# A hybrid RWKV/pooling layer on one core: block reads in four parts, one corner transposition, weights asked for seven tiles ahead

## The chip, the cores and the metric

The kernel runs on one core of one Trainium2 chip. The metric is the device time of one execution in microseconds; the median over runs is what is compared. Names used below: PE is TensorE (PEld its weight load), DVE is VectorE, ACT is ScalarE, POOL is GpSimd, SP is the sync engine, whose queue (SPq) issues nearly all transfers here; ACTq issues a few.

## The reference

One layer (DEPTH = 1) over 512 positions of width 2048, in float32:

```python
h = rms_norm(x, norm_g);  z = h @ w_in                  # 2048 -> 3200 + 1024 + 1024 + 1024 columns
zs = zs + (token_shift(zs) - zs) * mu                    # r, k, v, two low-rank inputs
decay = exp(-exp(-softplus(-(w0 + tanh(wd) @ w_up)) - 0.5));  a = sigmoid(a0 + ad @ a_up)
S_t = S_{t-1} (diag(w_t) - kk_t^T (a_t*kk_t)) + v_t^T k_t;  y_t = S_t r_t     # 16 heads x 64, 512 steps
y_rwkv = (head_group_norm(y) + bonus) * silu(g_rwkv)
y_pool = (trailing means over 2/4/8/16 - u) @ w_pool * pool_scale * silu(g_pool)
x = x + concat(y_rwkv, y_pool) @ w_out
x = x + sigmoid(x @ w_pg + b_pg) * (p @ w_ple)
out = rms_norm(x, final_g)
```

## The kernel before, in words

**Products.** Each large float32 product is made of three reduced-precision ones: `wsplit` reads a weight tile into `raw` (SP), ACT casts it to `whi` (line 132), DVE subtracts to get `wlo` (line 133), and PE multiplies `whi` by the high and the low part of the activations and `wlo` by the high part. The pools of `raw`, `whi` and `wlo` have four buffers each. One tile of `w_in` holds 4 x 128 rows by 128 columns and feeds 12 products of 512 columns.

**Weights' order.** `plan` lists all tiles in the order of use. `chunk(nm, c)` hands out one; each time it also calls `wsplit` for the two that follow it in `plan`. A scheduler in the compiler then sets the order on each engine: among what is ready it takes what the program wrote down first, except where `high_priority` lifts an instruction. PE keeps the program's order. `tc.issue_after(ins)` adds an order, without a wait, between `ins` and what the block puts on `ins`'s own engine.

**Stages.** First the norm and the transposition of x (to about 27 us). Then the middle stage (27 to 690 us): eight passes `j`, two heads each. In a pass, `recur(j)` walks eight chunks of 64 positions: the product `py` (state against queries), the sum `zs` on DVE, the product `pu`, copies `uv` on ACT, the product `ps`, the new state `sbd` on DVE. Between these links `pump` fills PE with the projections of the next passes and with the pool units (`zk`, `zr`, `zv`, `zg`, `zb`). Then the two projections with `w_out` and `w_pg` (690 to 1067 us) and the last norm.

**The block inverse.** While `recur(j)` runs, pass j+1 is prepared. After chunk 0, `scores(j + 1)` makes masked score blocks `mt`, writes the 32 x 32 diagonal blocks to DRAM (`nd`, four writes), and reads them back so that each of four groups of 32 partitions holds all of them: two tiles `n32`, rows 0 to 15 and rows 16 to 31 of the blocks, each with one read whose source is broadcast over four (line 682). Behind these on SP come the low-rank weights (`load_ab`), four reads of `bg` (128 KB each) and four of `vg` (64 KB each). `invert(j + 1)` solves the blocks in 31 short steps on DVE (`tm` line 709, `xw` line 713), two after each link from the second link of chunk 2 on; its first 16 steps need the first tile `n32` only. At its end it writes `xd` and reads it back into the corners of `x1` (four reads of 32 partitions, line 724).

**The corner.** `gather(j + 1)` turns the left half of `x1` in blocks of 32 x 32 on DVE, in two instructions of 32 partitions each (`y1`, line 777), and PE multiplies by the result (`pq`, 32 x 32 products). `turn_key` (chunk 7) needs `bg`, the transposition of `uv` in `gather` needs `vg`.

```python
        yt = [nc.vector.transpose(y1[pb:pb + 32], x1[pb:pb + 32, :, 0:32]) for pb in (0, 64)]
        ...
        units(lambda u, par, pb: mm(ps3[pb + 32:pb + 64, u, :],
                                                  mt[pb:pb + 32, par, u, 1 - par, 32:64],
                                                  y1[pb:pb + 32, u, :], start=True, stop=True,
```

Of the kernel before, what the change touches and what calls it, by code (L numbers as in the profile page):

```python
# [9 lines left out]
F32 = mybir.dt.float32  # L10
# [5 lines left out]
P = 128  # L16
# [8 lines left out]
NCH = T // C  # L25
# [9 lines left out]
def trunk_kernel(ctx: ExitStack, tc: tile.TileContext, x, p, norm_g, w_in, mu, w0, w_up, a0, a_up,  # L35
                 k_k, k_a, r_k, ln_w, ln_b, w_pool, pool_scale, w_out, w_ple, w_pg, b_pg, final_g, out):
    nc = tc.nc
    PSUM = bass.MemoryType.PSUM
    x, p, w_in, w_out, w_ple, w_pg = x[0], p[0, 0], w_in[0], w_out[0], w_ple[0], w_pg[0]
    out = out[0]  # L40
# [85 lines left out]

    def wsplit(src, kt, n, nm):
        raw = wp.tile([P, kt, n], F32, name=f"raw_{nm}", tag="raw")
        made = [nc.sync.dma_start(out=raw, in_=src)]
        hi = wp.tile([P, kt, n], F32R, name=f"whi_{nm}", tag="whi")  # L130
        lo = wp.tile([P, kt, n], F32R, name=f"wlo_{nm}", tag="wlo")
        made.append(nc.scalar.copy(hi, raw))  # L132
        made.append(nc.vector.tensor_tensor(lo, raw, hi.bitcast(F32), ALU.subtract))  # L133
        wmade[:] = made
        return hi, lo

    wmade = []

    def split(hi, lo, src):
        c_ = nc.scalar.copy(hi, src)  # L140
# [18 lines left out]
    def mm(*a, **k):  # L159
        i = nc.tensor.matmul(*a, **k)  # L160
        return tc.keep_in_program_order(i) if pin[0] else i
# [11 lines left out]
    plan, ready = [], {}  # L173
# [2 lines left out]
        for c in range(KT // CK):  # L176
            plan.append((nm, c, w_in[c * CK * P:(c + 1) * CK * P, c0:c0 + P].rearrange("(k p) n -> p k n", p=P), CK, P))

    def chunk(nm, c, ahead=2):
        while (nm, c) not in ready or ahead > 0:  # L180
            if (nm, c) in ready:
                ahead -= 1
            if not plan:
                break
            n_, c_, src, kt, w_ = plan.pop(0)
            if (n_, c_) not in ready:
                ready[n_, c_] = wsplit(src, kt, w_, f"{n_}_{c_}")
        return ready.pop((nm, c))

    yd = dram.tile([KT, P, T], F32, name="yd", bufs=1)  # L190
# [5 lines left out]
    n_ = 0  # L196
# [13 lines left out]
    for kind, nm, j in jobs:  # L210
# [7 lines left out]
        else:  # L218
            g, i = j // 4, j % 2
# [79 lines left out]
    for d in range(KT):  # L299
        xt_half(0, d)  # L300
        if d in WPOS:
            c = len(wl_)
# [18 lines left out]
    for g, win in enumerate(WINDOWS):  # L321
        t_ = cst.tile([P, win], F32, name=f"rc{g}")
# [21 lines left out]
    rw = s2a.enter_context(tc.tile_pool(name="rw", bufs=1))  # L344
# [6 lines left out]
    def load_ab(j):  # L351
        jc = slice(j * P, (j + 1) * P)
        w2 = []
        for nm, src in (("u", w_up), ("a", a_up)):
            raw = rw.tile([P, P], F32, name=f"{nm}r{j}", tag=f"l{nm}r")
            for h in range(2):
                nc.sync.dma_start(out=raw[64 * h:64 * h + 64, :], in_=src[0, :, jc])
            w2.append((raw, rw.tile([P, P], F32R, name=f"{nm}s{j}", tag=f"l{nm}s")))
        wab[j] = w2
# [24 lines left out]
    for nm, rows in (("u", slice(0, 64)), ("a", slice(64, 128))):  # L384
# [3 lines left out]
        t_ = rw.tile([P, T], F32R, name=f"{nm}hh")  # L388
# [10 lines left out]
    def zcols(ps, nm):  # L399
        for c in range(KT // CK):  # L400
            wh, wl = chunk(nm, c)
            for k in range(CK):
                kk = c * CK + k
                mm3(ps, wh[:, k, :], wl[:, k, :], hhi[:, kk, :], hlo[:, kk, :], kk == 0, kk == KT - 1)
                place[0] = 3 * (kk + 1)
                yield 3
# [107 lines left out]
                assert (nm, j) in zt  # L514
        return zt[nm, j]

    pws, kks, nrs, vgs, read, late = {}, {}, {}, {}, [], [None]

    H1, H2, H3, H4, H5, HE = 6, 12, 20, 8, 13, 40

# [34 lines left out]
    st_ = {}  # L555
# [3 lines left out]
    def prepare_key(j):  # L559
        k_ = need("k", j)  # L560
        kk = rw.tile([P, T], F32, name=f"kk{j}", tag="kk")
        nc.scalar.activation(kk, k_, AF.Square, scale=pc("k_k", j))
        kqh = rw.tile([P, T], F32R, name=f"kqh{j}", tag="t", bufs=4)
        kql = rw.tile([P, T], F32R, name=f"kql{j}", tag="t", bufs=4)
        split(kqh, kql, kk)
        kks[j] = (kk, kqh, kql)
# [25 lines left out]
    def scale_key(j):  # L592
        k_, kk = need("k", j), kks[j][0]
        if j < 2:
            nc.vector.reciprocal(kk, kk)
        nc.vector.scalar_tensor_tensor(kk, k_, pc("k_k", j), kk, ALU.mult, ALU.mult)
        kks[j] = kk
# [48 lines left out]
    def scores(j):  # L646
        ar, bk, v_ = (st_[j][n_] for n_ in ("ar", "bk", "v_"))
        kph, kpl = st_[j].pop("kp")

        mt = rw.tile([P, 2, 8, 2, C], F32, name=f"mt{j}", tag="mt", bufs=2)  # L650
        pm = [[psM.tile([P, T], F32, name=f"pm{j}_{par}0", tag="m"),
               psY.tile([P, T], F32, name=f"pm{j}_{par}1", tag="y")] for par in range(2)]
        for par in range(2):
            for q in range(4):
                for h in range(2):
                    rows = slice(64 * h, 64 * h + 64)
                    mm(pm[par][h][:, q * P:(q + 1) * P], bk[rows, q, 2 * par:2 * par + 2, :],
                       ar[rows, q, 2 * par:2 * par + 2, :], start=True, stop=True)
        for par in range(2):
            for h in range(2):  # L660
                nc.vector.tensor_tensor(mt[:, par, h::2, :, :],
                                        pm[par][h].rearrange("p (u a t) -> p u a t", u=4, a=2),
                                        msk[:, par:par + 2, :].unsqueeze(1).to_broadcast([P, 4, 2, C]), ALU.mult)


        ps = psM.tile([P, T], F32, name=f"pbo{j}", tag="m")
        mm(ps, blk, kph, start=True, stop=False)
        mm(ps, blk, kpl, start=False, stop=True)
        bv = rw.tile([P, T], F32, name=f"bv{j}", tag="bv", bufs=2)
        nc.vector.tensor_tensor(bv, ps, v_, ALU.mult)  # L670

        nd = dram.tile([2, 2, 8, 32, 32], F32, name=f"nd{j}", tag="nd")
        for par in range(2):
            pb = 64 * (1 - par)
            for b in range(2):
                rows = slice(pb + 32 * b, pb + 32 * b + 32)
                nc.sync.dma_start(out=nd[par, b].rearrange("u r c -> r u c"),
                                  in_=mt[rows, par, :, 1 - par, 32 * b:32 * b + 32])
        nb = []
        for i in range(2):  # L680
            t_ = rw.tile([P, 16, 32], F32, name=f"n32{j}_{i}", tag=("kk", "kp")[i])
            n_ = nc.sync.dma_start(out=t_, in_=nd[:, :, :, 16 * i:16 * i + 16, :].rearrange(
                "a b u r c -> (a b u) r c").unsqueeze(0).to_broadcast([4, 32, 16, 32]))
            nb.append(t_)
        if j + 1 < NJ:
            with tc.issue_after(n_.ins):
                load_ab(j + 1)
        bg = rw.tile([P, NCH, 4, 32], F32, name=f"bg{j}", tag="bk")
        with tc.issue_after(n_.ins):
            for q in range(4):  # L690
                nc.sync.dma_start(out=bg[32 * q:32 * q + 32],
                                  in_=st_[j]["bkd"].rearrange("(b k) (c q i) -> q k c b i", b=4, q=4, i=32)[q])
        if j:
            vg, vd = vgs[j]
            with tc.issue_after(n_.ins):
                for q in range(4):
                    nc.sync.dma_start(out=vg[32 * q:32 * q + 32],
                                      in_=vd.rearrange("(b k) (c q i) -> q k c b i", b=4, q=4, i=32)[q])
        st_[j].update(mt=mt, nb=nb, bv=bv, bg=bg)


# [28 lines left out]
    def gather(j):  # L730
# [8 lines left out]
        if j:  # L739
            vg, _ = vgs.pop(j)  # L740
# [26 lines left out]
        x1 = d["x1"]  # L767
# [6 lines left out]
        y1 = rw.tile([P, 8, 32], F32, name=f"y1{j}", tag="tm")  # L774

        with tc.issue_after(late[0].ins):
            yt = [nc.vector.transpose(y1[pb:pb + 32], x1[pb:pb + 32, :, 0:32]) for pb in (0, 64)]
        with tc.issue_after(yt[0].ins), tc.issue_after(yt[1].ins):
            if normed:
                normed.pop()()  # L780
            if j + 1 < NJ:
                scale_key(j + 1)
# [29 lines left out]
    def recur(j, work, between):  # L812
        d = st_.pop(j)
        pw, ar, mt, bv, uv, mv, x1 = (d[n_] for n_ in ("pw", "ar", "mt", "bv", "uv", "mv", "x1"))
# [5 lines left out]
        def step():  # L820
            hop[0] += 1
            if hop[0] > HS:
                with tc.issue_after(lead[0].ins):
                    for _ in range(HN + (hop[0] == HE1)):
                        next(work, None)
# [4 lines left out]
        for ch in range(NCH):  # L830
            par, q = ch % 2, ch // 2
            pb = 64 * (1 - par)
# [49 lines left out]
            if ch == NCH - 1:  # L882
                for c0 in range(0, NCH, 4):
                    py = pys[c0 // 4]
                    for qq in range(2):
                        for h in range(2):
                            for pr in range(2):
                                c_ = c0 + 2 * qq + pr
# [5 lines left out]
                    for pr in range(2):  # L894
                        yr = slice(64 * pr, 64 * pr + 64)
                        nc.scalar.copy(ysb[yr, c0 // 2:c0 // 2 + 2, :], py4[yr, pr::2, :])
            step()
            if j + 2 < NJ and ch == 4:
                prepare_key(j + 2)
            if ch == 0:  # L900
# [59 lines left out]
    prepare(0)  # L960
    pump(H3)
    scores(0)
    pump(H2)
    for _ in invert(0):
        pass
    pump(HT)
    gather(0)
    for j in range(NJ):
        def between():
# [5 lines left out]
        if j + 1 == NJ:  # L975
            pn.append(rw.tile([P, 2, T // 32, 32], F32, name="pn", tag="ar", bufs=2))
            for q in range(4):
                for c in range(2):
                    nc.sync.dma_start(out=pn[0][32 * q:32 * q + 32, c],
                                      in_=p[:, c * P + 32 * q:c * P + 32 * q + 32].rearrange("(b k) i -> k b i", k=32))  # L980
# [93 lines left out]
    for ec in range(D // EC):  # L1074
# [3 lines left out]
        for tt in range(NT):  # L1078
            rows = slice(tt * P, (tt + 1) * P)
            t_ = pp.tile([P, EC], F32, name=f"x2_{ec}_{tt}", tag=("u", "sw")[tt // 2])  # L1080
# [3 lines left out]
                                in_=t_.rearrange("p (c e) -> p c e", e=P))  # L1084
# [204 lines left out]
```

## Time and profile before

| what | value |
|---|---|
| median of 3 runs | 1072.54 us (1072.24 to 1074.22) |
| the profiled execution's own time | 1077.76 us |
| its span, first to last instruction | 1076.0 us |
| PE busy | 1047.7 us (97%) |
| DVE busy | 711.7 us (66%) |
| ACT busy | 435.0 us (40%) |
| mean granted TensorE clock | 0.997 |

The profile is one execution. A row of the timeline gives the start, the duration, the engine, the line and operation, what is written and read (without buffer numbers), how many alike were merged, and in brackets the idle time of the engine just before it and what ended that. A row of the waits gives the engine and line that waited, for whom, the total, the number of times and the longest. A row of the windows gives a stretch, the busy time of each engine in it with its instructions, the granted clock, the share of the 16 DMA engines that was busy, and GB/s.

### The profile page before, as it was taken

The page shows a single profiled execution, that of the slowest core. Times are in us where ns is not written, and L with a number is a line of the kernel's source. Part 1 is how long each engine was busy: PE and PEld are TensorE (multiplying, and loading weights), DVE is VectorE, ACT ScalarE, POOL GpSimd, SP SyncE. Part 2 cuts the span into 40 slices and gives each one's busy share as a digit, 9 for nine tenths or more (in the row PEclk, how much of TensorE's full clock was granted, in tenths as well). Part 3 has the DMA queues.
Part 4 walks back from the last instruction along what each step waited for, and adds up shares of the span by engine and source line. Part 5 has one row for each costly group of instructions (what it writes and reads, how often), then busy time and mean ns, then how long its engine had stood idle before and what let it go on. Part 6 is the DMA issues. An engine that isn't in the chain of part 4 may idle for free.

```text
span 1076.0 us, 17131 instructions
## 1 busy us (share of the span) xinstructions
PE 1047.7 (97%) x5912; PEld 864.6 (80%) x5912; DVE 711.7 (66%) x1879; ACT 435.0 (40%) x893; POOL 72.6 (7%) x180
## 2 busy tenths in 40 slices
PE   5999999999999999999999999999999999999996
PEld 4888878888877887888888788888888888888885
DVE  6676968878688689687786977464353344435356
ACT  7633424434334345253443344544232232324337
POOL 2100011010110110101101201000000000000000
PEclk9999999999999999999999999999999999999998
DMA  7434453453443544534544453775747659454534
GB/s 237 110 115 101 135 132 95 130 139 99 143 116 100 160 105 128 128 95 133 132 118 133 112 130 108 225 259 163 183 152 190 163 145 272 129 177 159 173 98 157
DMA packets 272733, 155.41 MB, mean 144 GB/s; under 512 B 114449, under 2 KB 235386, under 8 KB 272646
## 3 DMA queue, kind: packets, MB, share of 16 engines
q1 hardware_dynamic: 244630, 125.74, 42.2%
q10 hardware_dynamic: 28016, 28.58, 8.8%
q8 instruction: 46, 0.75, 0.3%
q14 instruction: 41, 0.34, 0.1%
HBM read 128.79 MB, written 24.95 MB: 143 GB/s over the span
## 4 chain that ended last, share of the span: by engine, by line
PE 81%; DVE 9%; DMA 5%; ACT 2%; issue 2%; SPq 1%; ACTq 0%; DVEq 0%
PE acc_o L160 16%; PE acc_g L160 16%; PE zb L160 10%; PE zv L160 7%; PE zr L160 7%; PE zg L160 6%; PE zk L160 6%; PE py L160 2%; PE pple L160 2%; DMA n<-nd 1%; PE pu L160 1%; PE pm L160 1%; DMA x<-xd 1%; PE pp L160 1%; PE ps L160 1%
## 5 line engine op out<-in xcount | busy, mean ns | idle before, releaser
L133 DVE TENSOR_TENSOR wlo_g<-raw_g,whi_g 128x512 fp32r<-128x512 f32 x84 | 57.1, 687 | 76.0 <-ACT whi_g L132 73.8
L160 PE MATMUL zb<-hhi,whi_b 128*128 128x512 f32 x256 | 105.5, 412 | 0.0
L160 PE MATMUL zb<-hhi,wlo_b 128*128 128x512 f32 x256 | 100.4, 392 | 0.0
L160 PE MATMUL zb<-hlo,whi_b 128*128 128x512 f32 x256 | 99.8, 390 | 0.0
L160 PE MATMUL acc_o<-wlo_o,yhi 128*128 128x512 f32 x256 | 99.6, 389 | 0.0
L160 PE MATMUL acc_o<-whi_o,ylo 128*128 128x512 f32 x256 | 99.6, 389 | 0.0
L133 DVE TENSOR_TENSOR wlo_o<-raw_o,whi_o 128x512 fp32r<-128x512 f32 x64 | 43.9, 690 | 81.0 <-ACT whi_o L132 72.8
L160 PE MATMUL acc_o<-whi_o,yhi 128*128 128x512 f32 x256 | 94.7, 389 | 0.0
L132 ACT CAST whi_g<-raw_g 128x512 fp32r<-128x512 f32 x84 | 51.9, 620 | 103.0 <-PE acc_g L160 57.4
L160 PE MATMUL acc_g<-whi_g,x2hi 128*128 128x512 f32 x208 | 81.1, 390 | 0.0
L160 PE MATMUL acc_g<-wlo_g,x2hi 128*128 128x512 f32 x208 | 81.0, 389 | 0.0
L160 PE MATMUL acc_g<-whi_g,x2lo 128*128 128x512 f32 x208 | 80.7, 390 | 0.0
L881 POOL TENSOR_SCALAR s0p<-sbd,pw 64x64 f32<-64x64 f32 x96 | 56.4, 587 | 336.6 <-DVE sbd L874 245.1
L132 ACT CAST whi_o<-raw_o 128x512 fp32r<-128x512 f32 x64 | 39.5, 621 | 96.1 <-PE acc_o L160 55.0
L132 ACT CAST whi_b<-raw_b 128x512 fp32r<-128x512 f32 x64 | 39.6, 620 | 75.9 <-PE zb L160 22.4
L713 DVE TENSOR_TENSOR xw<-xw,tm 128x60 f32<-128x60 f32 (+24 forms) x248 | 52.2, 210 | 7.1
L160 PEld LDWEIGHTS zb<-hhi,wlo_b 128*128 128x128 f32 x256 | 48.0, 188 | 10.8
L160 PEld LDWEIGHTS acc_o<-whi_o,ylo 128*128 128x128 f32 x256 | 48.1, 188 | 10.1
L160 PEld LDWEIGHTS acc_o<-whi_o,yhi 128*128 128x128 f32 x256 | 48.0, 188 | 10.0
L160 PEld LDWEIGHTS acc_o<-wlo_o,yhi 128*128 128x128 f32 x256 | 48.0, 188 | 9.9
L133 DVE TENSOR_TENSOR wlo_b<-raw_b,whi_b 128x512 fp32r<-128x512 f32 x64 | 43.7, 684 | 17.8 <-ACT whi_b L132 17.2
L160 PEld LDWEIGHTS zb<-hhi,whi_b 128*128 128x128 f32 x256 | 48.2, 188 | 8.6
(289 smaller groups left out, 2502.2 us busy)
## 6 DMA issues: line engine op xcount, KB each, us to landing
raw_b<-in_w_in_dram SPq DMA_DIRECT2D x64, 256.0 KB
raw_o<-in_w_out_dram SPq DMA_DIRECT2D x64, 256.0 KB
raw_g<-in_w_pg_dram SPq DMA_DIRECT2D x64, 256.0 KB
raw_k<-in_w_in_dram SPq DMA_DIRECT2D x32, 256.0 KB
raw_r<-in_w_in_dram SPq DMA_DIRECT2D x32, 256.0 KB
raw_v<-in_w_in_dram SPq DMA_DIRECT2D x32, 256.0 KB
raw_g<-in_w_in_dram SPq DMA_DIRECT2D x32, 256.0 KB
bkd<-bk SPq DMA_DIRECT2D x8, 512.0 KB
```

The costliest lines, as they stand in the source:

```text
L132: made.append(nc.scalar.copy(hi, raw))
L133: made.append(nc.vector.tensor_tensor(lo, raw, hi.bitcast(F32), ALU.subtract))
L160: i = nc.tensor.matmul(*a, **k)
L713: nc.vector.tensor_tensor(xw[:, 0:n_, s + 1:32], xw[:, 0:n_, s + 1:32], tm[:, 0:n_, 0:w_], ALU.add)
L881: nc.gpsimd.tensor_scalar(s0p[hc, :], nxt[hc, hc], pcn[hc], None, ALU.mult)
```

## The change

Four edits. (1) The read of each tile `n32` becomes four reads, one for each group of 32 partitions; only the first tile is read at once. (2) The second tile, `load_ab`, and the reads of `bg` and `vg` in pairs become portions: from pass 1 on, one is issued at the end of each chunk (chunks 1 to 6), all behind the first tile's last read on SP; in pass 0 they follow it directly. (3) `chunk` keeps the tile asked for and six more behind it in `ready`, so weights are written down seven tiles ahead in place of three, and each weight read is put behind the last entry of `read` on SP. `read` now also holds the last read of the first `n32` tile, beside the corners' reads. (4) The corner is turned by one instruction of 128 partitions.

```diff
     def wsplit(src, kt, n, nm):
         raw = wp.tile([P, kt, n], F32, name=f"raw_{nm}", tag="raw")
-        made = [nc.sync.dma_start(out=raw, in_=src)]
+        with tc.issue_after(read[-1].ins) if read else ExitStack():
+            made = [nc.sync.dma_start(out=raw, in_=src)]
...
-    wmade = []
+    wmade, read, portions = [], [], []
...
-    def chunk(nm, c, ahead=2):
-        while (nm, c) not in ready or ahead > 0:
-            if (nm, c) in ready:
-                ahead -= 1
-            if not plan:
-                break
+    LEAD = 6
+
+    def chunk(nm, c):
+        while plan and ((nm, c) not in ready or len(ready) <= LEAD):
             n_, c_, src, kt, w_ = plan.pop(0)
-            if (n_, c_) not in ready:
-                ready[n_, c_] = wsplit(src, kt, w_, f"{n_}_{c_}")
+            ready[n_, c_] = wsplit(src, kt, w_, f"{n_}_{c_}")
         return ready.pop((nm, c))
...
             t_ = rw.tile([P, 16, 32], F32, name=f"n32{j}_{i}", tag=("kk", "kp")[i])
-            n_ = nc.sync.dma_start(out=t_, in_=nd[:, :, :, 16 * i:16 * i + 16, :].rearrange(
-                "a b u r c -> (a b u) r c").unsqueeze(0).to_broadcast([4, 32, 16, 32]))
             nb.append(t_)
+
+        def n_read(i):
+            for q in range(4):
+                r_ = nc.sync.dma_start(out=nb[i][32 * q:32 * q + 32], in_=nd[:, :, :, 16 * i:16 * i + 16, :].rearrange(
+                    "a b u r c -> (a b u) r c"))
+            return r_
+
+        n_ = n_read(0)
+        read.append(n_)
+        bg = rw.tile([P, NCH, 4, 32], F32, name=f"bg{j}", tag="bk")
+
+        def blocks(dst, src, qs):
+            for q in qs:
+                nc.sync.dma_start(out=dst[32 * q:32 * q + 32],
+                                  in_=src.rearrange("(b k) (c q i) -> q k c b i", b=4, q=4, i=32)[q])
+
+        later = [lambda: n_read(1)]
         if j + 1 < NJ:
-            with tc.issue_after(n_.ins):
-                load_ab(j + 1)
...
+            later.append(lambda: load_ab(j + 1))
+        for qs in ((0, 1), (2, 3)):
+            later.append(lambda qs=qs: blocks(bg, st_[j]["bkd"], qs))
         if j:
             vg, vd = vgs[j]
+            for qs in ((0, 1), (2, 3)):
+                later.append(lambda qs=qs: blocks(vg, vd, qs))
+        for fn in later if j == 0 else ():
             with tc.issue_after(n_.ins):
...
+                fn()
+        portions[:] = [(n_, fn) for fn in later] if j else []
...
-            yt = [nc.vector.transpose(y1[pb:pb + 32], x1[pb:pb + 32, :, 0:32]) for pb in (0, 64)]
-        with tc.issue_after(yt[0].ins), tc.issue_after(yt[1].ins):
+            yt = nc.vector.transpose(y1, x1[:, :, 0:32])
+        with tc.issue_after(yt.ins):
...
             step()
+            if portions:
+                n_, fn = portions.pop(0)
+                with tc.issue_after(n_.ins):
+                    fn()
```

More of the change, by code (lines that the diff above doesn't have):

```diff
@@ L515, in need @@
         return zt[nm, j]
-    pws, kks, nrs, vgs, read, late = {}, {}, {}, {}, [], [None]
+    pws, kks, nrs, vgs, late = {}, {}, {}, {}, [None]
     H1, H2, H3, H4, H5, HE = 6, 12, 20, 8, 13, 40
@@ L681, in scores @@
             t_ = rw.tile([P, 16, 32], F32, name=f"n32{j}_{i}", tag=("kk", "kp")[i])
-            n_ = nc.sync.dma_start(out=t_, in_=nd[:, :, :, 16 * i:16 * i + 16, :].rearrange(
-                "a b u r c -> (a b u) r c").unsqueeze(0).to_broadcast([4, 32, 16, 32]))
             nb.append(t_)
-        if j + 1 < NJ:
-            with tc.issue_after(n_.ins):
-                load_ab(j + 1)
[L688 to L692, printed above, removed]
+        def n_read(i):
[11 more added lines that the diff above has]
+        later = [lambda: n_read(1)]
+        if j + 1 < NJ:
+            later.append(lambda: load_ab(j + 1))
+        for qs in ((0, 1), (2, 3)):
+            later.append(lambda qs=qs: blocks(bg, st_[j]["bkd"], qs))
         if j:
             vg, vd = vgs[j]
+            for qs in ((0, 1), (2, 3)):
+                later.append(lambda qs=qs: blocks(vg, vd, qs))
+        for fn in later if j == 0 else ():
             with tc.issue_after(n_.ins):
-                for q in range(4):
-                    nc.sync.dma_start(out=vg[32 * q:32 * q + 32],
-                                      in_=vd.rearrange("(b k) (c q i) -> q k c b i", b=4, q=4, i=32)[q])
+                fn()
+        portions[:] = [(n_, fn) for fn in later] if j else []
         st_[j].update(mt=mt, nb=nb, bv=bv, bg=bg)
```

## The prediction

> **What bounds the kernel now.** First the busy times by stage (the windows), then what PE waits for, then those places in the timeline.
>
> ```profile
> 0.00:27.00 27.00, 15.09 (x85) 12.38 (x86) 18.40 (x50) 20.69 (x48) 6.44 (x54) 1.00 0.75 236
> 27.00:690.00 663.00, 655.33 (x4141) 539.97 (x4142) 509.06 (x1503) 275.74 (x597) 66.12 (x126) 1.00 0.47 124
> 690.00:1067.00 377.00, 377.00 (x1689) 312.20 (x1687) 180.56 (x316) 134.64 (x241) 0.00 (x0) 1.00 0.59 174
> 1067.00:1076.00 9.00, 0.26 (x3) 0.06 (x1) 3.71 (x12) 3.92 (x8) 0.00 (x0) 0.66 0.38 138
> ```
>
> PE (first number behind the length) is the bound, and the granted clock is full. The opening's 11.9 us without PE and the tail's 8.7 lie before and behind everything that the diff touches; from 690 to 1067 PE never stops. So the change works on the 663.00 - 655.33 = 7.7 us of PE's idle time in the middle stage. Whatever it does to SP, ACT or DVE counts only through them. The waits of PE in that stage:
>
> ```profile
> PE py L160 <- DVE sbd L874: 3.1, 4, 1.6
> PE pq L160 <- DVE y L777: 2.0, 4, 0.7
> PE pu L160 <- DVE zs L844: 1.4, 3, 0.8
> PE pq L160 <- DVE sw L423: 0.4, 1, 0.4
> PE pq L160 <- DVE nt L153: 0.4, 1, 0.4
> ```
>
> Thirteen waits, all on DVE, none on a weight tile and none on ACT. Where they stand in time:
>
> ```profile
> 296.70 0.39 PE L160 MATMUL zk<-hlo,whi_k 128*128 128x512 f32 x1
> 296.93 0.39 PE L160 MATMUL zk<-hhi,wlo_k 128*128 128x512 f32 x1
> 298.92 0.38 PE L160 MATMUL py<-sbd,ar 128*128 128x128 f32 x1 [1.60 <-DVE sbd L874]
> 152.03 0.38 PE L160 MATMUL py<-sbd,ar 128*128 128x128 f32 x1 [0.70 <-DVE sbd L874]
> 154.32 0.38 PE L160 MATMUL pu<-zs,x 128*128 128x128 f32 x1 [0.40 <-DVE zs L844]
> 591.70 0.38 PE L160 MATMUL py<-sbd,ar 128*128 128x128 f32 x1 [0.55 <-DVE sbd L874]
> 121.09 0.28 PE L160 MATMUL pq<-y,mt 32*32 32x32 f32 x7 [0.32 <-DVE y L777]
> 267.05 0.22 PE L160 MATMUL pq<-y,mt 32*32 32x32 f32 x2 [0.36 <-DVE nt L153]
> 341.75 0.34 PE L160 MATMUL pq<-y,mt 32*32 32x32 f32 x9 [0.73 <-DVE y L777]
> 415.87 0.22 PE L160 MATMUL pq<-y,mt 32*32 32x32 f32 x2 [0.65 <-DVE y L777]
> 487.63 0.25 PE L160 MATMUL pq<-y,mt 32*32 32x32 f32 x4 [0.45 <-DVE sw L423]
> 635.35 0.22 PE L160 MATMUL pq<-y,mt 32*32 32x32 f32 x2 [0.31 <-DVE y L777]
> ```
>
> The first two rows start 0.23 us apart though each lasts 0.39: products overlap by 0.16, so each gap costs 0.16 more than its bracket says. The stage's loss is thus 7.7 + 13 x 0.16 = 9.8 us, the most that can come back. It has three parts. The four rows ending in `py` or `pu` here: 1.60 + 0.70 + 0.40 + 0.55 = 3.25, with overlap **3.9 us**. The six `pq` rows: 2.82, with overlap **3.8 us**. The rest: **2.1 us**.
>
> **The blocks' read (edit 1).** What held DVE before the first part is the read of the blocks:
>
> ```profile
> DVE tm L709 <- DMA n<-nd: 22.9, 8, 5.2
> 287.57 1.17 SPq L682 DMA_DIRECT2D n<-nd  x2
> 291.36 0.29 DVE L844 TENSOR_TENSOR zs<-py,mv 64x128 f32<-64x128 f32 x1 [0.31 <-PE py L160]
> 296.16 0.19 DVE L709 TENSOR_TENSOR tm<-i,n 128x31 f32<-128x31 f32 x1 [4.50 <-DMA n<-nd]
> 289.50:292.50 3.00, 3.00 (x15) 2.49 (x15) 1.78 (x4) 0.97 (x2) 1.26 (x2) 1.00 0.32 72
> 299.00:300.00 1.00, 1.00 (x6) 0.87 (x7) 0.87 (x6) 0.09 (x1) 0.40 (x1) 1.00 0.81 222
> ```
>
> DVE takes its queue in order. Its first inverse step stands at 291.7 and waits until 296.16; the state sums `sbd` are queued behind it, and `py` waits for them. All eight passes wait, 22.9 us in sum; PE notices in those where `pump` has too few products between the links. From the first issue to the first step are 8.6 us for 256 KB, and while the two reads move, a third of the engines is busy at 72 GB/s (second last row; its last number), against 0.81 and 222 GB/s ten microseconds later. So the transfer is slow through few engines, not through load.
>
> After, the tile is read by four transfers of 32 partitions. The nearest rows are the corners' four reads of 32 partitions each, in pass 0, and the DVE instruction that waits for them:
>
> ```profile
> 116.51 1.81 SPq L724 DMA_DIRECT2D x<-xd  x4
> 120.04 0.90 DVE L777 STREAM_TRANSPOSE y<-x 32x256 f32<-32x256 f32 x2 [1.19 <-DMA x<-xd]
> ```
>
> Four reads take 3.5 us from first issue to use. An `n` issue costs 1.17 / 2 = 0.59 against 1.81 / 4 = 0.45, so 0.13 x 4 = 0.5 more: 4.0 us in place of 8.6, or 4.6 earlier. The longest of the eight waits, 5.2, keeps 0.6, the others little. Bounds: the parts are no quicker, and the 3.9 us stay; or all 3.9 go. I take 3.6, near the end the corner reads point to, and leave 0.3 for a pass that still waits. What is late next is PE itself: without the wait, DVE waits for `py` and `ps`. SP pays 3 more issues here, 1.8 us, and 3 more for the second tile; it spends most of its time on waits for buffers, not on issuing.
>
> [...]
>
> **The portions (edit 2).** The second tile, `load_ab`, `bg` and `vg` move behind the first tile, and to the ends of chunks 1 to 6. Their users in the same pass:
>
> ```profile
> 318.89 0.29 DVE L844 TENSOR_TENSOR zs<-py,mv 64x128 f32<-64x128 f32 x1
> 325.05 0.70 DVE L643 STREAM_TRANSPOSE bkn<-bg 128x512 f32<-128x512 f32 x1
> 332.04 0.67 DVE L743 STREAM_TRANSPOSE uv<-vg 64x512 f32<-64x512 f32 x1
> 317.11 0.56 SPq L697 DMA_DIRECT2D vg<-vd  x1
> ```
>
> The `zs` at 291.36 above is that of chunk 2, the one at 318.89 that of chunk 6, so chunks are (318.89 - 291.36) / 4 = 6.9 us apart. The last `bg` pair goes out near the end of chunk 4, about 312, 13 us ahead of 325.05. The last `vg` pair goes out at the end of chunk 6, about 325, in place of 317.11; with 2 x 0.56 of issue and some 2 us of landing it is there at 328, 4 us ahead of 332.04. The second tile has from chunk 1 to step 16 (chunk 5), about 20 us. Cost: 0, covered by these 4 to 20 us; if the cover goes, DVE waits at `uv` or `bkn` as it did at `tm`, at most the few us by which it is late.
>
> **Weights (edit 3).** How early are they now? One tile, from read to product:
>
> ```profile
> 297.66 1.48 SPq L129 DMA_DIRECT2D raw_v<-in_w_in_dram  x2
> 306.10 0.62 ACT L132 CAST whi_v<-raw_v 128x512 fp32r<-128x512 f32 x1 [1.88 <-PE zr L160]
> 315.95 0.48 PE L160 MATMUL zv<-hhi,whi_v 128*128 128x512 f32 x1
> ```
>
> The read goes out 18.3 us before the product. One tile feeds 12 products of 0.23, 2.75 us, so that is 6.7 tiles ahead already: four `raw` and four `whi` buffers allow no more, and the cast waits for PE to free one. So asking seven tiles ahead brings no read forward. It does change rank: casts and `wlo` subtractions now stand ahead of what the program writes down in the 11 us between, and win ties on ACT and DVE. The tie on SP costs nothing while the blocks' reads hold SP for less than the 8.4 us between read and cast.
>
> **The corner (edit 4).** In pass 3:
>
> ```profile
> 338.70 0.43 DVE L777 STREAM_TRANSPOSE y<-x 32x256 f32<-32x256 f32 x1
> ...
> 340.59 0.69 DVE L133 TENSOR_TENSOR wlo_g<-raw_g,whi_g 128x512 fp32r<-128x512 f32 x1
> 341.27 0.42 DVE L777 STREAM_TRANSPOSE y<-x 32x256 f32<-32x256 f32 x1
> 263.65 0.43 DVE L777 STREAM_TRANSPOSE y<-x 32x256 f32<-32x256 f32 x1 [0.76 <-DMA x<-xd]
> ```
>
> PE waits for the second transposition (`pq` at 341.75), which stands 2.6 us behind the first with other work between. One instruction reads both corners, so it cannot stand earlier than the second's data allows; I put it at the second's place, with 0.43 less ahead of it. In the passes of 341, 415 and 487 that gives 3 x 0.43; in that of 267 also the 0.76 wait of the first goes, so its whole 0.36 + 0.16 = 0.5. In those of 121 and 635 the data itself is late: 0. Together **-1.8**. Bounds: all 3.8 gone; or, if it also waits for the two other reads, 0.45 later in eight passes, +3.6.
>
> **New order.** The rank of `wlo` and a DVE freed of 22.9 us of waiting change the order everywhere. The trace of before cannot show it. Bounds: the other 2.1 us vanish; or one subtraction of 0.69 falls before a link that PE needs in each of eight passes, +5.5. I take +1.0, near the lower end, since the links `zs` and `sbd` keep their lifted priority.
>
> **Sum.** -3.6 - 1.8 + 1.0 = -4.4 us. The profiled execution took 1077.76 us, 5.2 above the median; its differences are carried to the median: 1072.54 - 4.4 = **1068.1 us**.
>
> **Rivals.** *All waits go*: -9.8 us, 1062.7. For it speaks that all thirteen waits are on DVE; against, that any new order has its own. *No change*: the blocks land early, but the new order puts as many links late as it frees, 5.4 us of exposed work, eight subtractions of 0.69: 1072.5. For it: DVE is 77% busy in the stage (509.06 of 663). *Slower by rank*: subtractions with the higher rank stand ahead of the corner and the inverse's steps, two exposed in each of seven passes, 14 x 0.69 = 9.7, so -5.4 + 9.7 = +4.3, 1076.8; it decides above 11 exposed (7.5 us). Against it: each tile still has one subtraction, and they are spread. *Weights late*: SP is held by the blocks' writes and reads beyond 8.4 us, and PE waits about 2 us in seven passes: 1072.5 - 5.4 + 14 = 1081. Against it: 18.3 us of lead. *The parts are no quicker*: the edit doesn't do what it says, the 3.9 us stay, and with -1.8 + 1.0 it is 1071.7. The corner reads speak against it.
>
> [...]
>
> **How the numbers follow.** A measurement of this kernel tells 0.2%, 2.1 us, from no change. Chances: forecast (1063.5 to 1070.4) 0.55; all waits gone 0.10; no change, with the parts no quicker in it, 0.18; slower by rank 0.13; weights late 0.04. So faster 0.65, same 0.18, slower 0.17. The range 1063.0 to 1075.0 reaches over the first three and to the edge of the fourth.
>
> **What would show it.** Right: `tm <- n` under 4 us in place of 22.9; no `py` wait behind a first `tm`; `pq` waits near 1 us; the weight reads still about 18 us ahead. Wrong: PE waiting for `whi` or `wlo`, DVE waiting at `uv` for `vg`, or new `py` and `pu` waits of over 5 us with a subtraction just ahead of the link.

## The result, and the profile after

The changed kernel takes 1085.84 us (median of 4, 1085.32 to 1086.73) against 1072.82 (4 runs, 1072.24 to 1074.22): 1.2% slower, ratio 1.012 with a 95% interval of 1.0105 to 1.0136. The prediction said 1068.1 us and faster.

PE's waits in the middle stage (who waits for whom, us in total, times, longest):

```profile
PE zr L161 <- ACT whi_r L133: 6.7, 2, 3.5
PE zr L161 <- DVE wlo_r L134: 5.8, 1, 5.8
PE pyt L165 <- DVE ysb L939: 0.7, 1, 0.7
PE px L161 <- issue: 0.6, 1, 0.6
PE pu L161 <- DVE zs L855: 0.4, 1, 0.4
```

The waits named in the prediction are gone: no `py`, no `pq`, one `pu`. In their place stand three waits for a weight tile, 12.5 us in sum, all in pass 0. The same place in the timeline, first PE, then SP:

```profile
98.05 0.50 PE L161 MATMUL zr<-hhi,whi_r 128*128 128x512 f32 x1 [3.49 <-ACT whi_r L133]
104.56 0.80 PE L161 MATMUL zr<-hhi,wlo_r 128*128 128x512 f32 x1 [5.78 <-DVE wlo_r L134]
105.16 0.63 PE L161 MATMUL zr<-hhi,whi_r 128*128 128x512 f32 x1
105.58 0.63 PE L161 MATMUL zr<-hlo,whi_r 128*128 128x512 f32 x1
112.39 0.50 PE L161 MATMUL zr<-hhi,whi_r 128*128 128x512 f32 x1 [3.20 <-ACT whi_r L133]
```
```profile
81.99 3.57 SPq L684 DMA_DIRECT2D n<-nd  x8
...
88.10 2.86 SPq L694 DMA_DIRECT2D bg<-bkd  x4
91.00 1.22 SPq L130 DMA_DIRECT2D raw_r<-in_w_in_dram  x1
102.69 2.54 SPq L728 DMA_DIRECT2D xd<-xw  x4
106.65 1.81 SPq L735 DMA_DIRECT2D x<-xd  x4
108.50 1.55 SPq L130 DMA_DIRECT2D raw_r<-in_w_in_dram  x3
```
Before, the four reads of these `r` tiles went out ahead of, and between, pass 0's block reads:

```profile
74.71 2.56 SPq L129 DMA_DIRECT2D raw_r<-in_w_in_dram  x2
82.29 0.39 SPq L129 DMA_DIRECT2D raw_r<-in_w_in_dram  x1
82.86 1.19 SPq L682 DMA_DIRECT2D n<-nd  x2
85.01 0.39 SPq L129 DMA_DIRECT2D raw_r<-in_w_in_dram  x1
```

Now the first stands at 91.00, behind the block reads, and the other three at 108.50, behind the corners' reads, which wait for the whole inverse on DVE (SP stands still from 92.2 to 102.69). PE wants the first at 98.05 - 3.49 = 94.6. By then its transfer has ended (no DMA engine is busy from 94.4 to 98.0), but ACT casts the tile only at 97.38, behind three steps of the key. The longest wait, 5.78 us, is for the subtraction, which stands on DVE behind the rest of the inverse, whose last step is the first row here, and two transpositions:

```profile
102.45 0.17 DVE L724 TENSOR_TENSOR xw<-xw,tm 128x8 f32<-128x8 f32 x1
103.86 0.65 DVE L134 TENSOR_TENSOR wlo_r<-raw_r,whi_r 128x512 fp32r<-128x512 f32 x1
```

So a read that comes late costs once more in the queues of ACT and DVE. Whether a better place there alone, with the reads as late as here, would save these two waits was not run. The price is more than the waits: the rows at 105.16 and 105.58 start 0.42 us apart in place of 0.23.

```profile
98.00:104.50 6.50, 0.73 (x2) 0.30 (x2) 5.88 (x23) 0.00 (x0) 0.00 (x0) 0.60 0.03 5
104.50:108.50 4.00, 3.94 (x9) 3.14 (x10) 0.01 (x1) 0.00 (x0) 0.00 (x0) 0.50 0.25 41
112.40:116.20 3.80, 3.80 (x9) 2.80 (x10) 2.72 (x4) 1.86 (x3) 0.00 (x0) 0.57 0.78 216
```

The granted clock (in the windows the third number from the end) is 0.50 in the second window and 0.57 on the mean of the third. Ten products from 104.56 to 109.20 and nine from 112.39 to 116.27 take 8.5 us, where 19 at 0.23 and one overlap of 0.16 would take 4.5: 4 us too much. With 12.5 + 3 x 0.16 = 13 us of waits that makes 17 us. The medians differ by 13.0, so the other edits should be worth about -4 us; the experiments test that.

### The profile page after: what moved, and what is told of

It is laid out like the page before. It is cut to its first block, busy times and chain, and to the rows that moved or that the text cites. A ratio compares the mean times of both kernels' runs of the same rounds, so it can differ in the third digit from the quotient of the medians.

```text
span 1083.6 us, 17191 instructions
## 1 busy us (share of the span) xinstructions
PE 1048.7 (97%) x5912; PEld 866.3 (80%) x5912; DVE 709.5 (65%) x1871; ACT 436.9 (40%) x893; POOL 69.8 (6%) x180
## 4 chain that ended last, share of the span: by engine, by line
PE 92%; DVE 3%; ACT 2%; DMA 1%; SPq 1%; issue 1%; ACTq 0%; DVEq 0%
PE acc_o L161 16%; PE acc_g L161 16%; PE zb L161 15%; PE zv L161 8%; PE zk L161 8%; PE zr L161 8%; PE zg L161 7%; PE pple L161 2%; PE py L161 2%; PE pu L161 2%; PE pm L161 1%; PE ps L161 1%; PE pp L161 1%; PE pmv L161 1%; PE zl L161 1%; DMA xt<-in_x_dram 1%
## 5 line engine op out<-in xcount | busy, mean ns | idle before, releaser
L892 POOL TENSOR_SCALAR s0p<-sbd,pw 64x64 f32<-64x64 f32 x96 | 53.0, 552 | 333.5 <-DVE sbd L885 249.2
L161 PE MATMUL zr<-hhi,whi_r 128*128 128x512 f32 x128 | 54.8, 428 | 6.7 <-ACT whi_r L133 6.7
L161 PE MATMUL zr<-hhi,wlo_r 128*128 128x512 f32 x128 | 52.3, 408 | 5.8 <-DVE wlo_r L134 5.8
```

The costliest lines, as they stand in the source:

```text
L892: nc.gpsimd.tensor_scalar(s0p[hc, :], nxt[hc, hc], pcn[hc], None, ALU.mult)
```

## The experiments

Ratios are to the kernel before, measured beside it on the same chip, with the 95% interval. Three theories: **A**, the tie in pass 0 holds the weights back; **B**, the rank of casts and subtractions does it; **C**, the list rule does it, because the old rule asked for more than the new one, not less.

| kernel | median us | before beside it | ratio |
|---|---|---|---|
| before, profiled again | 1074.68 (one run) | 1074.88 | |
| parts alone | 1081.97 | 1074.88 | 1.0071 (1.0058 to 1.0084) |
| corner alone | 1072.72 | 1074.88 | 0.9979 (0.9967 to 0.9992) |
| changed, tie from pass 1 on | 1080.90 | 1074.88 | 1.0056 (1.0042 to 1.0069) |
| changed, growing list | 1070.56 | 1074.70 | 0.9962 (0.9948 to 0.9976) |
| changed, no tie | 1080.36 | 1074.70 | 1.0053 (1.0041 to 1.0066) |
| changed, list of eleven | 1079.52 | 1074.70 | 1.0044 (1.0031 to 1.0056) |
| before + list of seven + tie | 1121.71 | 1074.70 | 1.0438 (1.0423 to 1.0453) |
| changed, once more | 1085.38 | 1073.63 | 1.0105 (1.0092 to 1.0119) |
| changed, growing list in pass 0, then seven | 1068.48 | 1073.63 | 0.9952 (0.9938 to 0.9967) |
| changed, growing list, no tie | 1070.90 | 1073.63 | 0.9972 (0.9961 to 0.9983) |
| before + list of seven | 1109.39 | 1073.63 | 1.0330 (1.0314 to 1.0345) |
| changed, tie from pass 1 on, pass 0's reads spread | 1069.23 | 1074.75 | 0.9947 (0.9932 to 0.9962) |

**Before, profiled again.** 

> The kernel before, profiled once more. The profiled execution of before stood 5.2 us above the median of its runs, that of after 0.5 below its median, so the spans differ by 7.6 us and the medians by 13.0. If the first profile of before was a slow draw, this one has a span near 1071 to 1072 us and shows which waits were extra in the first. If profiling costs before 5 us each time, the span is again near 1076.

Its span is 1073.0 us, and its time of 1074.68 is in line with the 1074.88 of the runs beside it. PE's waits in the middle stage and DVE's wait for the blocks:

```profile
PE pq L160 <- DVE y L777: 1.8, 3, 0.7
PE pu L160 <- DVE zs L844: 1.1, 2, 0.8
PE py L160 <- DVE sbd L874: 1.0, 2, 0.7
PE pq L160 <- DVE sw L423: 0.5, 1, 0.5
```
```profile
  DMA n<-nd: 19.0, 7
```

So the first profile was a heavy draw: 4.4 us of PE waits here, 7.3 there, and only 1.0 in place of 3.1 at `py`. What the blocks' read costs PE varies between executions.

**Tie from pass 1 on.** 

> The changed kernel with one difference: weight reads are tied behind the blocks' and corners' reads from pass 1 on only; in pass 0 they are free. Theory A (the tie in pass 0 holds back the reads of tiles r of pass 1, at 91.0 and 108.5 us, and PE starves from 94 to 116 us): the reads go out near 75 to 85 us again, the 13.2 us of waits there go, the 4 us of slow clock behind them too, and the time is 1085.8 - 17 = about 1068 us (1065 to 1071), below before. Theory B (the seven tiles' rank puts the inverse's steps ahead of the subtractions, and the tie is innocent): the waits at 94 to 116 us stay, 1080 us or more.

```diff
-        with tc.issue_after(read[-1].ins) if read else ExitStack():
+        with tc.issue_after(read[-1].ins) if len(read) > 5 else ExitStack():
```

Half of the loss against before goes, ratio 1.0056; theory A alone is not enough. Three reads of `r` go out by 82.07 now, but the fourth is still late:

```profile
88.80 3.15 SPq L694 DMA_DIRECT2D bg<-bkd  x4
105.19 2.54 SPq L728 DMA_DIRECT2D xd<-xw  x4
107.83 0.55 SPq L130 DMA_DIRECT2D raw_r<-in_w_in_dram  x1
```
```profile
PE zr L161 <- ACT whi_r L133: 9.0, 1, 9.0
```

**Parts alone.** 

> The kernel before with the blocks' two reads in four parts each, nothing else. The prediction's first term, -3.6 us: near 1069 us, DVE's wait for the blocks under 5 us in place of 22.9, and no py wait behind a first inverse step. Rival: the parts land as late as the single read and the time stays at 1072 to 1073; or the first profile's waits were a slow draw, DVE's wait shrinks and the time still moves by less than 2 us.

```diff
-            n_ = nc.sync.dma_start(out=t_, in_=nd[...].unsqueeze(0).to_broadcast([4, 32, 16, 32]))
+            for q in range(4):
+                n_ = nc.sync.dma_start(out=t_[32 * q:32 * q + 32], in_=nd[...])
```

Slower by 0.7%. Its waits, DVE's on the blocks and PE's:

```profile
  DMA n<-nd: 3.4, 6
```
```profile
PE pss L160 <- ACT kqh L140: 4.0, 6, 1.7
PE pss L160 <- DVE kql L141: 2.0, 6, 0.4
PE py L160 <- DVE sbd L875: 0.2, 1, 0.2
```

The parts are quick: 22.9 and 19.0 us of DVE's waiting become 3.4, and the `py` wait shrinks to 0.2. But six passes now wait at `pss` (a product with the key), 6.0 us in sum, for the key's split `kqh` and `kql` on ACT and DVE; before, there was no wait there. The same four reads within the whole change bring no `pss` wait, so it is the order around them that does it; why the scheduler chose it is not shown.

**Corner alone.** 

> The kernel before with one corner transposition in place of two, nothing else. The prediction's second term, -1.8 us: near 1071 us, with the pq waits at 1 to 2 us in place of 2.8. Rival: the one instruction waits for all four corner reads and stands later, 0 to +3.6 us, 1072.5 to 1076.

```diff
-            yt = [nc.vector.transpose(y1[pb:pb + 32], x1[pb:pb + 32, :, 0:32]) for pb in (0, 64)]
+            yt = nc.vector.transpose(y1, x1[:, :, 0:32])
```

2.2 us faster (ratio 0.9979), near the forecast's 1.8. That it comes from the corner is not shown. The waits at `pq` are 1.5 us in sum here, 2.3 in the second profile of before; but those at `py` and `pu` are 2.7 in place of 2.1, and the first product with `w_out`, where the middle stage ends, starts at 711.64 here and at 711.40 there (716.29 in the first profile). The 1.6 us between these two profiled executions arise behind that point, 350.7 us to the last product against 352.5, in a stage that the edit does not touch.

**The growing list put back.** 

> The changed kernel with the list rule of before put back: each call writes down two more tiles than it hands out, so the list grows ahead of PE; all else as changed, the tie too. Theory C (the new rule does not ask earlier: before, the list had grown to some twenty tiles by pass 0; seven is less, and so the reads of tiles 20 to 23 fall behind pass 0's block reads and the whole inverse): the wait at 94 to 116 us goes, with its slow clock, 17 us less than the changed kernel, ratio to before 0.993 to 0.999. Theory B (rank of the casts and subtractions): with the higher rank back, waits of pss on kqh return as in the kernel with the parts alone, 6 us, ratio 1.000 or more.

```diff
-        while plan and ((nm, c) not in ready or len(ready) <= LEAD):
+        while (nm, c) not in ready or ahead > 0:
+            if (nm, c) in ready:
+                ahead -= 1
...
```

The whole loss goes: 1070.56 us, ratio 0.9962, and the `pss` wait that theory B expected does not return. The tie is still there, but these reads were written down before there was anything to tie them to:

```profile
81.58 0.39 SPq L130 DMA_DIRECT2D raw_r<-in_w_in_dram  x1
82.16 1.29 SPq L687 DMA_DIRECT2D n<-nd  x3
84.30 0.39 SPq L130 DMA_DIRECT2D raw_r<-in_w_in_dram  x1
```

**No tie.** 

> The changed kernel without any tie of the weights, list of seven kept. Theory C: as with the tie from pass 1 on, one long wait of 9 us near 102 to 111 us stays, because the fourth read of r stands behind the inverse's writes though nothing ties it there; ratio 1.004 to 1.007. Theory A (the tie alone): no wait there, ratio 0.997 or less.

```diff
-        with tc.issue_after(read[-1].ins) if read else ExitStack():
-            made = [nc.sync.dma_start(out=raw, in_=src)]
+        made = [nc.sync.dma_start(out=raw, in_=src)]
```

Ratio 1.0053, one wait of 9.1 us at `zr`: the same as with the tie from pass 1 on. So against the kernel before, the tie in pass 0 costs about half of the loss. Against the growing list (0.9962) it costs about two fifths, as the ratio goes from 1.0105 and 1.0120 in two measurements to 1.0053, and the short list without it costs the rest.

**List of seven and tie alone.** 

> The kernel before with the third edit alone: list of seven and the tie behind the blocks' and corners' reads; reads of blocks whole, two corner transpositions. Theory C with A: the first read of r stands behind pass 0's block reads (about 91 us) and the second behind the corners' reads (about 117 us, the inverse being as slow as before), so PE is without weights from 97 to 121 us but for one tile: 18 to 22 us of waits and 4 us of slow clock, ratio 1.018 to 1.026. Theory B (rank only): within 5 us of before.

The third edit's lines on the kernel before. 4.4% slower, twice what I expected: pass 0 starves much as foreseen, with 16.3 us of waits, and each later pass waits 1.6 to 3.6 us more for `whi` and `wlo`, which I had not foreseen.

**List of eleven.** 

> The changed kernel with eleven tiles in the list in place of seven. Theory C: tiles 20 to 24 are read before the inverse ends, tile 25 only behind the corners' reads at about 108 us; PE wants it at 94.5 + 5 x 2.75 = 108.3 us and gets it at 108 + 4.5, one wait of about 4 us and 0 to 4 us of slow clock, so 9 to 13 us less than the changed kernel, ratio 0.999 to 1.004. Theory B: no dependence on the length, ratio near 1.012.

```diff
-    LEAD = 6
+    LEAD = 10
```

```profile
106.81 2.55 SPq L728 DMA_DIRECT2D xd<-xw  x4
112.71 1.55 SPq L130 DMA_DIRECT2D raw_v<-in_w_in_dram  x3
```
```profile
PE zv L161 <- ACT whi_v L133: 4.4, 2, 3.1
PE zv L161 <- DVE wlo_v L134: 1.7, 1, 1.7
```

Four more tiles move the starvation by four tiles, from `r` to `v`, and halve it: 6.1 us of waits, ratio 1.0044, just above the range that C gave. The length of the list sets where PE runs dry.

**Changed, once more.** 

> The changed kernel once more, beside the three below on one chip. All theories: ratio 1.010 to 1.014, with the waits on r's tiles between 94 and 116 us again, so that they are no accident of one profile.

Ratio 1.0105, with the same three waits at `zr`, 12.5 us in sum, and the same mean granted clock of 0.992 in the profiled execution.

**List of seven alone.** 

> The kernel before with the list of seven alone, no tie, reads whole, two transpositions. Theory C: the fourth read of r falls behind four block reads (about 93 us in place of 85.0) but ahead of the inverse's writes, and PE wants it at 102.7: no wait, ratio 0.997 to 1.003. If the short list is harmful by itself, through the rank of casts and subtractions: ratio 1.004 or more.

My expectation was wrong: 3.3% slower, not unchanged. PE already waits 6.9 us in pass 0, where I expected none. In pass 1 SP shows why:

```profile
149.34 0.39 SPq L129 DMA_DIRECT2D raw_r<-in_w_in_dram  x1
149.91 1.19 SPq L679 DMA_DIRECT2D n<-nd  x2
153.63 7.11 SPq L688 DMA_DIRECT2D bg<-bkd  x4
160.78 2.95 SPq L694 DMA_DIRECT2D vg<-vd  x4
163.82 1.67 SPq L129 DMA_DIRECT2D raw_r<-in_w_in_dram  x3
```
```profile
PE zr L160 <- DVE wlo_r L133: 10.7, 4, 5.1
PE zr L160 <- ACT whi_r L132: 4.8, 4, 1.8
```

Three reads of `r` stand behind ten block reads, 14 us after the one before them; three casts then run in a row at 174.00, and waits of this kind, on `r`, `v` or `b` tiles, recur in every later pass. With the list grown long these reads were written down before the block reads and went out between them (in pass 1 of before at 140.84, 144.49, 151.37 and 153.17). With seven they come after, and the whole row goes first. The changed kernel, with the same short list but the portions of the second edit from pass 1 on, has no wait for a weight tile in those passes. So the portions are what a short list needs, and pass 0 has none.

**Growing in pass 0, then seven.** 

> The changed kernel with the list of before (growing) through pass 0, and the list of seven from pass 1 on. Theory C (all the loss is pass 0's): no wait in pass 0, as with the growing list, and in passes 1 to 7 the changed kernel's 2.4 us of lost PE time in place of 5.1 with the growing list: 2 to 3 us below that one, ratio 0.992 to 0.996. Rival: the list of seven costs in later passes as well once pass 0 is not late, ratio 0.998 or more.

```diff
+        goal = len(ready) + 2 if first[0] else LEAD + 1
-        while plan and ((nm, c) not in ready or len(ready) <= LEAD):
+        while plan and ((nm, c) not in ready or len(ready) < goal):
...
```

1068.48 us, ratio 0.9952. The first product with `w_out` starts at 706.48 us, in the changed kernel at 723.78: 17.3 us, the 17 reckoned above. Three waits are left in the middle stage:

```profile
PE pyt L165 <- DVE ysb L941: 0.7, 1, 0.7
PE px L161 <- issue: 0.6, 1, 0.6
PE pu L161 <- DVE zs L857: 0.4, 1, 0.4
```

**Growing list, no tie.** 

> The changed kernel with the growing list and no tie. If the tie holds nothing once the list is long, since the reads were written down before the entry they would be tied to: the same as with the tie, ratio 0.994 to 0.999. If the tie is what keeps the blocks' and corners' reads early, 2 us or more above it, ratio 0.998 to 1.001.

Ratio 0.9972 (0.9961 to 0.9983) against 0.9962 (0.9948 to 0.9976) with the tie: the intervals overlap, so no worth of the tie is shown.

**Pass 0's reads spread, list of seven kept.** 

> The changed kernel with the tie from pass 1 on, the list of seven throughout, and pass 0's other reads no longer in one row behind the blocks' first tile: the second tile at once, the low-rank weights and the four bg reads after half of the products that follow the inverse. If pass 0 starves because these reads stand in one row ahead of the weights and SP then waits for the inverse (the kernel with the tie from pass 1 on, one wait of 9.0 us), the reads of r's fourth tile and v's first two now stand ahead of them: that wait goes, ratio 0.995 to 0.999. If a short list starves pass 0 whatever stands in between: a wait of 5 us or more stays, ratio 1.003 or more.

```diff
-        for fn in later if j == 0 else ():
-            with tc.issue_after(n_.ins):
-                fn()
-        portions[:] = [(n_, fn) for fn in later] if j else []
+        portions[:] = [(n_, fn) for fn in later]
+        if j == 0:
+            fn0 = portions.pop(0)[1]
+            with tc.issue_after(n_.ins):
+                fn0()
...
-    pump(HT)
+    pump(HT // 2)
+    while portions:
+        n_, fn = portions.pop(0)
+        with tc.issue_after(n_.ins):
+            fn()
+    pump(HT // 2)
```

The tie begins with pass 1 here too. 1069.23 us, ratio 0.9947. The list is as short as in the changed kernel and the wait is gone:

```profile
82.48 3.62 SPq L684 DMA_DIRECT2D n<-nd  x8
86.19 0.39 SPq L130 DMA_DIRECT2D raw_r<-in_w_in_dram  x1
87.30 3.09 SPq L130 DMA_DIRECT2D raw_v<-in_w_in_dram  x2
94.05 3.13 SPq L694 DMA_DIRECT2D bg<-bkd  x4
```

So a short list starves PE where block reads stand in one row ahead of the weights, not by itself. Nor does PE wait for any `wlo` here, though the short list gives the subtractions the rank that they have in the changed kernel: once the reads go out early, no wait for a weight tile is left for theory B to explain. This version and the one that grows in pass 0 and then keeps seven beat both kernels; their intervals overlap.

## Why the prediction was wrong

**The step that failed is the one on the third edit.** I read `ahead=2` as two tiles ahead, and wrote, in the account of the code too, that three became seven. Each call of `chunk` hands out one tile and writes down two new ones, so the list grows by one with each call: by tile 20 it was some twenty long. Seven was fewer, not more. Both sentences built on it fail. "Asking seven tiles ahead brings no read forward" is true but misses that it puts reads back. And the place of the weights in the order fell where I let it rise: before, the subtractions of pass 1's four `r` tiles stand on DVE among the steps of the inverse, at 92.53, 96.55, 99.46 and 102.61; in the changed kernel the first stands behind the last step, at 103.86, though its cast ends at 97.99. (PE runs its 5912 products in the same order in both profiles.) So the rival *slower by rank* had its sign wrong; the list of seven alone, 3.3% slower, shows how much that place was worth. The term that I put at nothing cost 17 us: 13 of waits and 4 of slow clock.

**"The tie on SP costs nothing while the blocks' reads hold SP for less than the 8.4 us between read and cast"** was the right test, not carried out. In pass 0 the reads behind the tie stand from 91.00 to 108.50, 17.5 us, because the corners' reads are in the same `read` list and the inverse follows the scores at once there. I looked at pass 3, where recurrence and portions lie between. *Weights late* was the rival that came true, in one pass and not in seven; 0.04 was far too little, and 1081 us too low, since the clock's fall was not in it. That its seven waits of 2 us come to 14, near the 13 of the three waits that there were, is luck.

**The rest of the sum came out, but not term by term.** The sum for all edits but the weights' loss was -4.4 us. The growing list put back gives -4.1 (1070.56 - 1074.70), growing then seven -5.1, the spread reads -5.5. By terms: the corner is -2.2 against -1.8, for a reason that the traces do not show. The blocks' parts: DVE's wait went as said, from 22.9 to 3.4, but alone they cost 7.1 us through `pss`, which is the *new order* term, put at +1.0 and bounded at +5.5. So the near agreement of the sum is in part luck. "The parts are no quicker" is ruled out. Why they are quicker is not shown: that the single read is slow "through few engines" was my reading of a share of 0.32 at 72 GB/s, but no view here counts the engines of one transfer, and while four parts go out in pass 2 of the profile after (228.25 to 231.25) the share is 0.33 at 90 GB/s. The portions cost nothing that shows: DVE waits for neither `bg` nor `vg` in the profile after. That they are worth a great deal once the list is short I did not see. The 2 us put for the landing of a `vg` read were an estimate that no row of such a read shows; the nearest one, the corners' reads in pass 0 of before, has 1.7 us from the end of the last issue (118.32) to the use (120.04).

**The profile taken was a heavy draw.** Its 3.1 us at `py` were 1.0 in a second execution, so the first term was sized on a wait that varies. The two best versions still gain 5 us, and most of that comes from the other waits: where I left 2.1 us and added 1.0, three waits of 1.7 us in sum are left in all. With 0.16 for each wait, 5.8 us of lost PE time in the second profile of before become 2.2; the first product with `w_out` comes 4.9 us earlier.

## What to carry to other kernels

When a loop writes down prefetches, count how the list grows over many calls; do not read its depth off a parameter. An order tie, or a row of transfers on one queue, is priced where the cover is thinnest: here in the first pass, where what it stands behind, a whole inverse, has nothing between and the tied reads go out 17.5 us apart. The starved TensorE cost the waits, 13 us, and 4 us more of slow clock behind them.

## What the runs showed of the hardware

That the granted clock would halve behind the waits I had not counted: 0.42 us from product to product in place of 0.23 at a granted clock of 0.50. In windows of 0.1 us in the profile after, it falls to 0.50 at 99.25, only 0.5 us into the wait of 5.8 us; it is back at 1.00 at 109.5, falls again at 112.9, 0.5 us after PE has its tile, and is back at 116.3. So at the first fall the wait of 3.5 us lay behind it, and the two products between the waits ran at 1.00 (98.0 to 99.2). The four changes lie 10.2, 3.4 and 3.4 us apart. PE worked 0.7 us of the 3.4 before 99.25, and 0.5 us of the 3.4 before 112.9. What sets these times is not shown. In the first profile of before, where PE's longest wait in the middle stage is 1.6 us, the clock stands at 1.00 from 27 to 690 us. Over whole profiled executions, the mean granted clock is 0.978 to 0.994 in the seven with waits for weight tiles of 6.1 us or more in sum, and 0.997 or 0.998 in the two of before, the parts, the corner, the growing list, the list that grows in pass 0 and then keeps seven, and the spread reads, where the middle stage has no such wait.

A transfer whose source is broadcast over four held DVE 19 to 23 us over the passes, and four transfers of 32 partitions with the same bytes, in the kernel with the parts alone, 3.4.
